# One attention-score kernel: the first of twelve input loads made in two transfers, rows 0 to 111 and rows 112 to 127

## The chip, the core and the metric

The kernel runs on one core of a Trainium2 chip. The metric is the device time of one execution in microseconds (us), the median of several runs; lower is better. The profile is one execution recorded by the hardware profiler.

## The reference

```python
def reference(x, y):      # x, y: (8, 12, 512, 64) float32
    return np.einsum('bhtc,bhsc->bhts', x, y).astype(np.float32)
```

For each of 96 heads, the 512 x 64 matrix x is multiplied by the transpose of the 512 x 64 matrix y. The output has 96 matrices of 512 x 512 in float32. 25.2 MB are read and 100.7 MB are written.

## The kernel before, in words

The 96 heads are taken in six groups of 16 (NG = 6). A group's x, and likewise its y, is one tile of 128 partitions by 4096 floats: 128 rows of 16 KB, 2 MB, contiguous in memory. So there are twelve loads, x and y in turn (load n is x of group n // 2 for even n, y for odd n). There are 48 outputs of 2 MB, each a tile of the same shape, 128 x 4096 floats. Loads and outputs share five slots in SBUF (`slots`, line 61); a slot is handed out in turn by `slot()` (line 123).

Each group goes through these steps:

- `load(n)` (line 127) issues the transfer of one tile into a slot on SyncE's DMA queue (line 131).
- `compress(n)` (line 136) casts it to bf16: x by one copy on ACT into `xk`, y by four copies on DVE, POOL and ACT into `yb`.
- `mix` (line 160) arranges x in `xb`, `transposes` (line 175) turns both in blocks of 32 x 32 on DVE, into `xT` and `yT`.
- `products` (line 197) makes four matmuls into half of PSUM, and `result` (line 221) copies each half to the output's slot, nearly always on ACT.
- `store` (line 211) sends the slot out, every third output (and the last four) on ACT's queue and the others on SyncE's.

All is written by hand in one order, and `emit` (line 86) adds the waits. It keeps for each buffer who wrote it last and who has read it since, and has the next instruction wait on those semaphores. A DMA into or out of slot i counts on the slot's own semaphore, `dma{i}`, which rises by 16 with each transfer (`step`, line 93); a reader waits for the count that stood after the last write. `writes=both(i)` is what makes a load the writer of both halves of slot i.

Near the change the order is this: lines 246 and 247 issue loads 0 to 4 back to back on SyncE, into the five empty slots. Nothing is waited for. Then two memsets, and `compress(0)`, the first reader of slot 0, on ACT (line 113 within `copy`). When load 0 is compressed, load 5 goes into slot 0, and so on. The loop of line 255 does the twelve loads; the first outputs are made in between.

At the end, line 278 has five engines wait for the last transfers of the five slots.

Of the kernel before, what the change touches and what calls it, by code (L numbers as in the profile page):

```python
# [9 lines left out]
def kernel(  # L10
# [22 lines left out]
    nc = tc.nc  # L33
    B, H, T, C = x.shape
    _, _, S, _ = y.shape
    P = 128
# [16 lines left out]
    xv = x.rearrange("b h t c -> (b h t c)").rearrange("(g p n) -> g p n", p=P, n=R * C)  # L53
    yv = y.rearrange("b h t c -> (b h t c)").rearrange("(g p n) -> g p n", p=P, n=R * C)
# [6 lines left out]
    slots = [sb.tile([P, K * S], fp32, name=f"slot{i}") for i in range(SLOTS)]  # L61
# [9 lines left out]
    def need(name, points):  # L71

        best = {}
        for p, v in points:
            if known[name].get(p, 0) < v:
                best[p] = max(best.get(p, 0), v)
        for p, v in list(best.items()):
            if any(snaps[q, w].get(p, 0) >= v for q, w in best.items() if q != p):
                del best[p]
        for p, v in best.items():  # L80
            engines[name].wait_ge(sems[p], v)  # L81
            known[name][p] = v
            for q, w in snaps[p, v].items():
                known[name][q] = max(known[name].get(q, 0), w)

    def emit(name, make, reads=(), writes=(), dma=None):

        points = [writer[r] for r in (*reads, *writes) if r in writer]
        points += [v for w in writes for v in readers.get(w, ())]
        if name == "pool" and name in ticks:  # L90
            points.append((name, ticks[name]))
        need(name, points)
        p, step = (name, 1) if dma is None else (f"dma{dma}", 16)
        if p not in sems:
            sems[p] = tc.alloc_semaphore(p)
        make().then_inc(sems[p], step)
        at = (p, ticks.get(p, 0) + step)
        ticks[p] = at[1]
        snaps[at] = {**known[name], p: at[1]}
        if dma is None:  # L100
            snaps[at][name] = at[1]
        for r in reads:
            readers.setdefault(r, []).append(at)
        for w in writes:
            writer[w], readers[w] = at, []
# [14 lines left out]
    def both(i):  # L120
        return [("slot", i, 0), ("slot", i, 1)]

    def slot():
        made_slots.append(len(made_slots) % SLOTS)
        return made_slots[-1]

    def load(n):
        i = loaded[n] = slot()
        emit(
            "sp",  # L130
            lambda: nc.sync.dma_start(slots[i], (yv if n % 2 else xv)[n // 2]),  # L131
            writes=both(i),
            dma=i,
        )

    def compress(n):

# [107 lines left out]
    with tc.tile_critical():  # L245
        for g in range(SLOTS):
            load(g)
        for half, name in enumerate(("dve", "pool")):
# [3 lines left out]
                writes=[("xb", half, part) for part in range(4)],  # L252
            )
        front = []
        for n in range(2 * NG):
            if n == 11:
                result(3, slot())
            compress(n)
            mix(n // 4, "pool", n % 4)
            if n == 4:  # L260
                transposes(0)
            if n < 5:
                load(n + SLOTS)
            elif n in (6, 8):
                load(n // 2 + 7)
            elif n < 10:
                front.append(slot())
            if n > 7 and n < 11:
                result(n - 8, front[n - 8])
            if n == 9:  # L270
                transposes(1)
# [38 lines left out]
```

## Time and profile before

| | |
|---|---|
| time, median of 3 runs | 300.91 us (300.87 to 301.03) |
| span of the profiled execution, first to last instruction | 299.3 us |
| ACT busy | 204.2 us, 68% |
| DVE busy | 160.8 us, 54% |
| PE busy | 131.2 us, 44% |
| POOL busy | 56.0 us, 19% |
| moved by DMA | 125.90 MB, 421 GB/s over the span |
| the loads, issue to landing | median 17.6 us (x), 20.8 us (y) |
| the stores, issue to landing | median 17.0 us (SyncE's queue), 14.8 us (ACT's) |

The profile gives the span of the recorded execution; the time that the runs report includes 1.6 us more around it (300.91 less 299.3). The page cuts the span into 40 slices of 7.48 us, and gives for each the busy tenths of every engine, the mean busy share of the core's 16 DMA engines and the GB/s that they moved. A window does the same for any stretch; a packet that the DMA engines move is booked in the window in which it starts, so a share can stand above 1. "SPq" and "ACTq" are the instructions with which SyncE and ACT issue a transfer. Behind the views, the trace keeps the start and the duration of each DMA packet (here one packet is one row of 16 KB), and the times at which the semaphore of a slot rose. Times are counted from the start of the span.

### The profile page before, as it was taken

What the parts mean: (1) busy time and instruction counts of PE and PEld (TensorE: products, weight loads), DVE (VectorE), ACT (ScalarE), POOL (GpSimd) and SP (SyncE); (2) the same over time, 40 slices, a digit from 0 to 9 for tenths busy, and PEclk for the clock granted to TensorE, in tenths of its full rate; (3) what the DMA queues carried; (4) which work ended last, traced back from release to release, by engine and by line L of the source; (5) the groups of instructions that cost most, each with busy time, mean ns of one, the idle gap of its engine ahead of it and who ended that gap; (6) DMA issues with size and microseconds to landing.
All of it is one profiled execution on the core that took longest, in us unless ns stands there. A gap on an engine that the chain in (4) does not pass through costs nothing.

```text
span 299.3 us, 1170 instructions
## 1 busy us (share of the span) xinstructions
PE 131.2 (44%) x384; PEld 35.2 (12%) x384; DVE 160.8 (54%) x77; ACT 204.2 (68%) x105; POOL 56.0 (19%) x23
## 2 busy tenths in 40 slices
PE   0000040557756665454655545464646473755100
PEld 0000010111111111111111111111111111111000
DVE  2167897999839590940946729219276330501400
ACT  1665676999999885677776868595959595459000
POOL 2399999991000000000000000000000000000000
PEclk9999999999599978596859597959597959587755
DMA  7999999999999999999999999999999999999995
GB/s 272 429 427 434 431 425 427 429 431 427 434 434 429 429 431 428 431 434 431 427 434 428 429 434 429 429 427 436 425 425 429 427 434 423 425 423 429 431 431 239
DMA packets 8645, 125.90 MB, mean 421 GB/s; under 512 B 960, under 2 KB 960, under 8 KB 960
## 3 DMA queue, kind: packets, MB, share of 16 engines
q1 hardware_dynamic: 6048, 88.08, 69.3%
q10 hardware_dynamic: 2592, 37.75, 29.6%
q8 instruction: 3, 0.05, 0.1%
q14 instruction: 2, 0.02, 0.0%
HBM read 25.17 MB, written 100.66 MB: 420 GB/s over the span
## 4 chain that ended last, share of the span: by engine, by line
DMA 57%; ACT 22%; PE 7%; issue 4%; DVE 3%; SPq 0%; ACTq 0%
DMA out_dram<-slot 44%; ACT slot L113 19%; DMA slot<-in_y_dram 7%; PE pm L202 7%; DMA slot<-in_x_dram 6%; DVE yb L115 2%; DVE slot L115 1%; ACT xk L113 1%; ACT yb L113 1%; SPq L131 0%; ACTq L81 0%; SPq L305 0%; SPq L245 0%
## 5 line engine op out<-in xcount | busy, mean ns | idle before, releaser
L113 ACT ACTIVATE slot<-pm 128x2048 f32<-128x2048 f32 x92 | 166.6, 1883 | 50.1 <-DMA out_dram<-slot 40.8
L202 PE MATMUL pm<-yT,xT 128*128 128x512 bf16 x384 | 131.2, 485 | 146.6 <-ACT slot L113 108.6
L180 DVE STREAM_TRANSPOSE xT<-xb 128x2048 uint32<-128x2048 uint32 x12 | 46.7, 3890 | 71.0 <-PE pm L202 68.6
L202 PEld LDWEIGHTS pm<-yT,xT 128*128 128x128 bf16 x384 | 35.2, 112 | 242.1 <-ACT slot L113 141.4
L115 DVE COPY xb<-xk 32x2048 bf16<-32x2048 bf16 x36 | 46.9, 1304 | 1.0
L115 DVE CAST yb<-slot 64x2048 bf16<-64x2048 f32 x12 | 36.1, 3012 | 17.0 <-DMA slot<-in_y_dram 16.8
L115 POOL COPY xb<-xk 32x2048 bf16<-32x2048 bf16 x12 | 36.2, 3019 | 10.5 <-ACT xk L113 9.7
L113 ACT ACTIVATE xk<-slot 128x4096 bf16<-128x4096 f32 x6 | 21.7, 3617 | 16.4 <-DMA slot<-in_x_dram 16.4
L115 DVE COPY slot<-pm 128x2048 f32<-128x2048 f32 x4 | 9.0, 2286 | 29.3 <-PE pm L202 29.3
L189 DVE STREAM_TRANSPOSE yT<-yb 128x1024 uint32<-128x1024 uint32 x12 | 23.2, 1932 | 0.0
L113 ACT ACTIVATE yb<-slot 64x2048 bf16<-64x2048 f32 x6 | 14.8, 2461 | 5.1 <-DMA slot<-in_y_dram 5.1
L115 POOL CAST yb<-slot 64x2048 bf16<-64x2048 f32 x6 | 17.8, 2968 | 1.3 <-DMA slot<-in_y_dram 0.8
L251 DVE MEMSET xb<- 128x2048 uint32 x1 | 1.8, 1765 | 1.4 <-SPq L245 1.4
L251 POOL MEMSET xb<- 128x2048 uint32 x1 | 1.8, 1804 | 0.5 <-SPq L245 0.5
L113 ACT ACT_TABLE_LOAD x1 | 1.3, 1283 | 0.9 <-SPq L245 0.9
L294 POOL MEMSET const-float32-0.0<- 128x1 f32 x1 | 0.1, 98 | 0.2 <-issue 0.2
L294 POOL MEMSET const-float32-1.0<- 128x1 f32 x1 | 0.1, 98 | 0.0
L294 POOL MEMSET const-bfloat16-1.0<- 128x1 bf16 x1 | 0.1, 98 | 0.0
L294 POOL MEMSET const-uint8-127<- 128x1 uint8 x1 | 0.1, 97 | 0.0
## 6 DMA issues: line engine op xcount, KB each, us to landing
out_dram<-slot SPq DMA_DIRECT2D x30, 2048.0 KB, 17.0
out_dram<-slot ACTq DMA_DIRECT2D x18, 2048.0 KB, 14.8
slot<-in_x_dram SPq DMA_DIRECT2D x6, 2048.0 KB, 17.6
slot<-in_y_dram SPq DMA_DIRECT2D x6, 2048.0 KB, 20.8
```

The source lines that it names most:

```text
L113: lambda: nc.scalar.activation(dst, src, COPY)
L115: else engines[name].tensor_copy(dst, src),
L180: lambda: nc.vector.transpose(xTs[half].rearrange("p (k r e) -> p k e r", k=K, e=E), xbs[half].rearrange("p (k e c) -> p k e c", k=K, e=E),),
L189: lambda: nc.vector.transpose(yTs[half].rearrange("p (r j) -> p j r", r=D), ybs[half][b].rearrange("p (j c) -> p j c", c=D),),
L202: last = nc.tensor.matmul(pms[k // 4][:, j, :], xT[:, k + j, h, :], yT[:, h * S:(h + 1) * S], start=True, stop=True,)
L251: lambda: engines[name].memset(xbs[half], 0.0),
L294: nc = _bacc.Bacc("TRN2", target_bir_lowering=False, num_devices=1)
```

## The change

Load 0 is made in two transfers on the same queue and with the same semaphore, rows 0 to 111 (14 of 16 parts of the tile, 1.75 MB) and rows 112 to 127 (256 KB). Only the second is marked as the slot's writer; since the semaphore then stands at 32, `compress(0)` waits for both. The eleven other loads are as before.

```diff
     def load(n):
         i = loaded[n] = slot()
-        emit(
-            "sp",
-            lambda: nc.sync.dma_start(slots[i], (yv if n % 2 else xv)[n // 2]),
-            writes=both(i),
-            dma=i,
-        )
+        edges = (0, 7 * P // 8, P) if n == 0 else (0, P)
+        for lo, hi in zip(edges, edges[1:]):
+            emit(
+                "sp",
+                lambda: nc.sync.dma_start(slots[i][lo:hi], (yv if n % 2 else xv)[n // 2, lo:hi]),
+                writes=both(i) if hi == P else [],
+                dma=i,
+            )
```

## The prediction

> **What bounds the kernel now.** I read the page's slices first, then the DMA table, the windows over the first microseconds, the order of time there, and the list of the DMA queue's own waits. The two DMA lines of the slices:
>
> ```profile
> DMA  7999999999999999999999999999999999999995
> GB/s 272 429 427 434 431 425 427 429 431 427 434 434 429 429 431 428 431 434 431 427 434 428 429 434 429 429 427 436 425 425 429 427 434 423 425 423 429 431 431 239
> ```
>
> The 16 DMA engines are busy from the second slice to the last but one, at 423 to 436 GB/s, whatever the other engines do. The busiest of those, ACT, is at 68%. So the end is set by bytes: 125.9 MB at some 430 GB/s. The trace's records of single packets say the same for one engine: 480 data packets of 16 KB, nearly all of 608 to 621 ns, median 611, each starting as the one before it ends. 480 x 0.61 us is 293 us, and the packets run from 1.98 to 297.84 us. Only three things can move the time: when full speed begins, what one engine's 480 packets take, and the few us after the last of them. A delay to one engine's packets early on is never made good, for its later packets queue behind it without a hole; it reaches the end whole if that engine is among the last to finish.
>
> The start is the one stretch below full speed that the change touches. In the windows the last two numbers are the DMA share and GB/s, both booked where a packet starts:
>
> ```profile
> 2.00:2.25 0.25, 0.00 (x0) 0.00 (x0) 0.25 (x1) 0.18 (x1) 0.25 (x1) 1.00 4.44 786
> 2.25:2.50 0.25, 0.00 (x0) 0.00 (x0) 0.25 (x1) 0.00 (x0) 0.25 (x1) 1.00 0.71 131
> 2.50:2.75 0.25, 0.00 (x0) 0.00 (x0) 0.25 (x1) 0.00 (x0) 0.25 (x1) 1.00 0.79 131
> 2.75:3.00 0.25, 0.00 (x0) 0.00 (x0) 0.25 (x1) 0.00 (x0) 0.00 (x0) 1.00 0.32 66
> 3.00:3.25 0.25, 0.00 (x0) 0.00 (x0) 0.21 (x1) 0.00 (x0) 0.00 (x0) 1.00 0.24 66
> 3.25:3.50 0.25, 0.00 (x0) 0.00 (x0) 0.00 (x0) 0.00 (x0) 0.00 (x0) 1.00 0.00 0
> 3.50:4.50 1.00, 0.00 (x0) 0.00 (x0) 0.00 (x0) 0.00 (x0) 0.00 (x0) 1.00 1.01 426
> ```
>
> Sixteen first packets start between 1.98 and 2.45, four engines start a second one before 3.03, and then none starts until 3.50; from there on the rate is full. In the packet records those first packets took 712 to 1956 ns in place of 611, and four second ones 959 to 1673. The first load lands at 8.79 us by its semaphore, 6.81 us after the first packet; the next lands 4.87 us later. So some 1.9 us are lost at the start, a ceiling for what any change there can gain.
>
> **The order around the change.** SyncE hands out the five loads like this (columns: start, duration, queue, line):
>
> ```profile
> 0.95 0.39 SPq L131 DMA_DIRECT2D slot<-in_x_dram  x1
> 1.40 0.42 SPq L131 DMA_DIRECT2D slot<-in_y_dram  x1
> ...
> 1.86 0.43 SPq L131 DMA_DIRECT2D slot<-in_x_dram  x1
> 2.33 0.66 SPq L131 DMA_DIRECT2D slot<-in_y_dram  x1
> 3.04 0.49 SPq L131 DMA_DIRECT2D slot<-in_x_dram  x1
> 8.81 3.62 ACT L113 ACTIVATE xk<-slot 128x4096 bf16<-128x4096 f32 x1 [6.63 <-DMA slot<-in_x_dram]
> ```
>
> **The change part by part.**
>
> *One more issue on SyncE.* The first issue is cut in two and the four other loads are pushed back by one issue, 0.39 to 0.66 us by these rows. SyncE's next instruction is the load at 12.46, which waits for ACT's xk, so the queue absorbs it. The DMA engines have the 112 rows, some 7 x 0.61 = 4.3 us of work each, before they need the next transfer; the second issue is out within 0.7 us. Nothing waits. If that cover were gone the cost would be one issue, 0.4 us.
>
> *An earlier start.* The first packet comes 0.63 us after the end of the first issue. If issue time goes with rows, 112 rows save an eighth of 0.39 us, 0.05 us. If it does not, nothing. I take zero.
>
> *16 more completion packets,* one for each engine. Their records are 7 to 9 ns, and a load's spacing of 4.87 to 4.89 us is 8 x 0.607 = 4.86 us of rows (packets overlap by about 4 ns) plus 0.01 to 0.03. I take +0.03 us.
>
> *The wait for load 0.* ACT's compress now waits for both transfers. Behind it on ACT stand the other copies; POOL's first mix waits for ACT's xk. If load 0 lands d later, slot 0 comes free d later and the load issued at 12.46 comes d later. It is needed only when the four loads behind are through, at 28.34 us by their semaphore: 15.9 us of cover. The tightest later place is 51.59, where a load is issued while transfers to 57.7 are still queued: 6 us of cover, and the delayed transfers shift with it. So the wait costs nothing by itself.
>
> *How the rows fall on the engines.* This is the disputed part. A 128-row transfer gives each engine 8 rows; they run without hindering one another, else 611 ns would not be the time of nearly every packet at all skews. 112 rows are 7 each and 16 rows are 1 each, so the bytes per engine are as before, if the division is even. But the 16 rows are neighbours, partitions 112 to 127 of one tile, and all 16 engines write them at about the same time as soon as they are through with their seven. The trace has no 16-row transfer. Bounds: nothing, if writes to neighbouring rows don't hinder one another (0.61 us for the row, which engine and row had before); and all sixteen one after another, 16 x 0.61 = 9.8 us, so +9.2. Below nothing: at most the 1.9 us of the slow start, if the other division of rows dissolves it. The nearest row is the one moment at which sixteen engines start together on one transfer and do hinder one another, the first packets: the slowest took 1956 ns, as if 3.2 engines shared one way. The end belongs to the slowest engine, so I take 1.956 - 0.611 = **+1.35 us** for the second transfer, as an estimate from that row.
>
> The Trainium skill speaks against the change here: "SBUF — State Buffer", section "Door 1: The DMA port swizzle (why `[64,N]` ≈ `[32,N]`)", says that a transfer's rate goes with how many of 16 ports its partitions reach, and has 104 GB/s for sixteen partitions, which reach four. By that the 256 KB would take 2.52 us in place of 0.61, +1.91 us, and the time would be 302.9 (an estimate from that page). The page measured a transfer by itself; no run here shows it yet, and the 611 ns of the 128-row transfers neither bear it out nor speak against it.
>
> The same doubt hangs on the seven-row shares. In the best case they fall as before and cost nothing; if engines met in twos for all seven rows, it would be 7 x 0.61 = +4.3 us. Full-speed packets of every 128-row transfer are the nearest row, so I take nothing and keep the upper end.
>
> *Sum:* 0 (issue) + 0 (start) + 0.03 + 0 (wait) + 1.35 + 0 = +1.38 us. Against the profiled execution's span of 299.3 that is 300.7. The median of the runs, 300.91, is 1.6 us above the span; what lies around the span does not change, so the forecast is 300.91 + 1.38 = **302.3 us**.
>
> **The rivals.**
>
> *A. It costs next to nothing.* The rows land as before, only the issue and the completions are added. For it: equal bytes for each engine, and a queue that is never empty. The upper end: the start's stall ends at 3.50 and SyncE's last issue at 3.53; if the stall is caused by the issues, a sixth makes it 0.42 us longer. Against that: the issue at 12.46 slows no packet. 300.9 to 301.4, middle 301.1.
>
> *B. Faster.* The first sixteen packets of a 128-row transfer hinder one another, 1.9 us lost in all. If that comes from which rows the engines start on together, shares of seven begin at other addresses and could be rid of it. It decides as soon as it returns more than the second transfer costs. Price: half of 1.9 us, 299.9 us. Against it: the stall ends for all engines at nearly one moment, 3.5, which looks like a start-up cost that any first transfer pays.
>
> *C. Seven-row shares collide too.* Half of the 4.3 us above, beside the 1.35: 304.4 us. For it: the change makes all shares start at uneven rows. Against it: engines out of step avoid one another after a collision.
>
> *D. The change does nothing on the chip* is out: the order of instructions has both transfers on SyncE and is otherwise the same on every engine.
>
> **How the numbers follow.** Forecast (301.6 to 303.2): 0.48. A: 0.24. B: 0.18. C and beyond: 0.10. Within 0.2% of 300.91 is 300.31 to 301.51, about what a measurement of this kernel can tell from no change; so faster 0.18, same 0.24, slower 0.58. The range goes from 300.0, which holds A and the edge of B, to 304.4, the middle of C; outside are some 0.14 of B and 0.05 of C.
>
> **What would show it.** In the changed profile the first load's landing, and so the start of ACT's first xk, moves from 8.81 to about 10.2; the windows between 6 and 10 us hold a dip to a quarter or a half of 430 GB/s; the last slices keep their 423 to 436 and the span grows by what the dip lost. If ACT still starts at 8.8 with a longer span, the row step is wrong. If the windows from 2.25 to 3.50 fill up, B is right. A first slice unchanged and a changed tail would mean that the end is set by something that I do not see.

## The result and the profile after

The changed kernel takes **304.67 us** (median of 4 runs, 304.63 to 305.29) against 300.97 (4 runs, 300.87 to 301.21) for the kernel before: +3.70 us, a ratio of 1.0126 (95% interval 1.0114 to 1.0138). The sign was forecast, the size was not: the forecast was 302.3, and the range ended at 304.4.

The span of the profiled execution goes from 299.3 to 302.8 us. Its slices, DMA share and GB/s:

```profile
DMA  7999999999999999999999999999999999999996
GB/s 214 307 426 424 431 431 428 428 426 433 428 437 428 433 426 425 439 422 428 433 428 420 436 426 418 437 422 428 433 426 424 435 424 420 437 420 426 435 422 260
```

The first slice has 214 GB/s where it had 272, the second 307 where it had 429; from the third on the rate is what it was. The share still says 9 in that slice: the DMA engines are busy, but their packets take longer. Everything that was lost was lost before 15 us. The windows over the start of the changed kernel (the last two numbers are DMA share and GB/s; "..." stands for lines left out):

```profile
2.25:2.50 0.25, 0.00 (x0) 0.00 (x0) 0.25 (x1) 0.00 (x0) 0.25 (x1) 1.00 0.00 0
...
3.25:3.50 0.25, 0.00 (x0) 0.00 (x0) 0.00 (x0) 0.00 (x0) 0.00 (x0) 1.00 0.83 328
3.50:4.50 1.00, 0.00 (x0) 0.00 (x0) 0.00 (x0) 0.00 (x0) 0.00 (x0) 1.00 1.16 344
4.50:8.50 4.00, 0.00 (x0) 0.00 (x0) 0.00 (x0) 0.00 (x0) 0.00 (x0) 1.00 1.03 274
8.50:12.50 4.00, 0.00 (x0) 0.00 (x0) 0.00 (x0) 0.00 (x0) 0.00 (x0) 1.00 0.90 221
```

The last two of these windows in the kernel before:

```profile
4.50:8.50 4.00, 0.00 (x0) 0.00 (x0) 0.00 (x0) 0.00 (x0) 0.00 (x0) 1.00 0.99 422
8.50:12.50 4.00, 0.00 (x0) 0.00 (x0) 0.00 (x0) 3.62 (x1) 0.01 (x1) 1.00 1.00 430
```

Here the whole of load 0 is slow, not only its last eighth: 274 GB/s while the seven-row shares are written (422 before), 221 while the 16 rows follow and load 1 begins (430 before). In the packet records, the packets that start between 3.5 and 8.3 us take 971 ns in the median, those between 8.3 and 11.3 us 1300; the kernel before has a median of 611 in both stretches. The excess over 611 ns of all data packets that start before 14 us, divided by 16 engines, is 4.15 us; it was 0.97. That is +3.2 us for the mean engine; the last packet of all ends 3.55 us later than before (301.39 against 297.84).

The records also show how many rows each engine had. A packet starts some 4 ns before the one ahead of it on its engine ends, so starts and ends can be linked into chains. In the changed kernel this gives sixteen chains, and each begins with seven packets of 16 KB and one completion packet. In fourteen of them one row and its completion follow as plainly; in the other two the second completion can't be told from a neighbour's. The shares are even, and the time went into slower packets, not into an engine with more rows than the others.

What followed on the other engines, in order of time:

```profile
0.95 0.86 SPq L133 DMA_DIRECT2D slot<-in_x_dram  x2
...
1.86 0.42 SPq L133 DMA_DIRECT2D slot<-in_y_dram  x1
2.32 0.74 SPq L133 DMA_DIRECT2D slot<-in_x_dram  x1
3.10 0.52 SPq L133 DMA_DIRECT2D slot<-in_y_dram  x1
3.67 0.46 SPq L133 DMA_DIRECT2D slot<-in_x_dram  x1
12.87 3.62 ACT L113 ACTIVATE xk<-slot 128x4096 bf16<-128x4096 f32 x1 [10.69 <-DMA slot<-in_x_dram]
16.52 0.33 SPq L133 DMA_DIRECT2D slot<-in_y_dram  x1
```

ACT's first copy moves from 8.81 to 12.87, and the load that follows it from 12.46 to 16.52, 4.06 us each. No hole opens behind them.

### The profile page after: what moved, and what is told of

Read it like the earlier page. It is cut to its first block, busy times and chain, and to the rows that moved or that the text cites. A ratio compares the mean times of both kernels' runs of the same rounds, so it can differ in the third digit from the quotient of the medians.

```text
span 302.8 us, 1164 instructions
## 1 busy us (share of the span) xinstructions
PE 126.7 (42%) x377; PEld 34.8 (11%) x384; DVE 161.3 (53%) x77; ACT 204.0 (67%) x105; POOL 56.2 (19%) x23
## 4 chain that ended last, share of the span: by engine, by line
DMA 56%; ACT 21%; PE 6%; DVE 5%; issue 4%; SPq 1%; ACTq 0%; DVEq 0%
DMA out_dram<-slot 41%; ACT slot L113 19%; DMA slot<-in_y_dram 8%; PE pm L204 6%; DMA slot<-in_x_dram 6%; DVE yb L115 2%; DVE slot L115 1%; DVE xT L182 1%; ACT xk L113 1%; ACT yb L113 1%; SPq L133 1%; DVE yT L191 1%; ACTq L81 0%; SPq L307 0%; DVEq L81 0%
## 5 line engine op out<-in xcount | busy, mean ns | idle before, releaser
L204 PE MATMUL pm<-yT,xT 128*128 128x512 bf16 x377 | 126.7, 475 | 154.7 <-ACT slot L113 106.4
```

Of the source, the lines that this page charges most:

```text
L204: last = nc.tensor.matmul(pms[k // 4][:, j, :], xT[:, k + j, h, :], yT[:, h * S:(h + 1) * S], start=True, stop=True,)
```

## The experiments

The theory after the result: a transfer's rate is set by which partitions of the tile it writes. Engines that write neighbouring partitions at the same time share a way into the SBUF and slow one another. Its rivals: (1) a second or a short transfer costs as such; (2) the addresses that are read, or uneven shares of seven rows (the chains above speak against the uneven shares); (3) the slow start of the first transfer. Each ratio is taken against runs of the kernel before that were made beside it (medians 300.95 to 301.00).

### Cut by columns in place of rows

```diff
-        edges = (0, 7 * P // 8, P) if n == 0 else (0, P)
+        edges = (0, 7 * K * S // 8, K * S) if n == 0 else (0, K * S)
...
-                lambda: nc.sync.dma_start(slots[i][lo:hi], (yv if n % 2 else xv)[n // 2, lo:hi]),
-                writes=both(i) if hi == P else [],
+                lambda: nc.sync.dma_start(slots[i][:, lo:hi], (yv if n % 2 else xv)[n // 2][:, lo:hi]),
+                writes=both(i) if hi == K * S else [],
```

> Load 0 is again made in two transfers of seven eighths and one eighth of its bytes, but cut by columns: both have all 128 rows. Theory (which partitions a transfer names decides; neighbouring ones share a way into the SBUF): no dip, the rows fall as in the kernel before, +0.03 to +0.1 us for one more row start and completion per engine: 300.9 to 301.4. Rival 1 (a second transfer in the first load, or a short one, costs as such): as the changed kernel, 304.0 to 305.0. Rival 2 (shares of seven rows begin at unlucky addresses in the memory that is read): 300.9 to 301.4 too, since every engine has 8 rows.

Measured: **300.94 us**, ratio 1.0000 (0.9991 to 1.0009). The same two transfers of seven eighths and one eighth cost nothing when both have all 128 rows. Rival 1 falls: neither the sixth issue, nor 16 completions more, nor a transfer of one eighth of the bytes costs anything that can be measured here.

### Two halves of 64 rows

```diff
-        edges = (0, 7 * P // 8, P) if n == 0 else (0, P)
+        edges = (0, P // 2, P) if n == 0 else (0, P)
```

> Load 0 in two transfers of 64 rows: four rows for each engine, twice. Theory: all rows of the first transfer lie in one half of the tile, so engines meet in twos at least on every row, 8 x 0.61 = +4.9 us at most: 304.7 to 305.9, not less than the changed kernel. Rival 1 (an extra transfer, the shorter the worse): less than the changed kernel, 301 to 303. Rival 2 (uneven shares of seven rows): about as before, 300.9 to 301.5. The Trainium skill, SBUF - State Buffer, section on Door 1, has partitions 0 to 63 reach half of the ports, which makes it +4.9 by that page (an estimate).

Measured: **305.74 us**, +4.79, ratio 1.0155 (1.0140 to 1.0170); above the change, though the shares are even and neither piece is short. Its windows:

```profile
4.00:6.00 2.00, 0.00 (x0) 0.00 (x0) 0.00 (x0) 0.00 (x0) 0.00 (x0) 1.00 1.04 213
6.00:8.00 2.00, 0.00 (x0) 0.00 (x0) 0.00 (x0) 0.00 (x0) 0.00 (x0) 1.00 0.89 197
8.00:10.00 2.00, 0.00 (x0) 0.00 (x0) 0.00 (x0) 0.00 (x0) 0.00 (x0) 1.00 1.19 246
10.00:12.00 2.00, 0.00 (x0) 0.00 (x0) 0.00 (x0) 0.00 (x0) 0.00 (x0) 1.00 0.83 172
```

The rate is about half of 430 GB/s for as long as load 0 lasts, and the packets that start from 3.8 to 11 us take 1279 ns in the median, 2.09 x 611, as if engines met in twos on every row. Eight rows at twice the time would be 8 x 0.61 = +4.9 us; the excess of the packets before 14 us is 5.15 us per engine against 0.97, so +4.2. Another 0.35 us has a different source: an issue of 64 rows takes 0.59 us in place of 0.39, and the first packet starts at 2.33 us in place of 1.98.

By the Trainium skill ("SBUF — State Buffer", section "Door 1: The DMA port swizzle (why `[64,N]` ≈ `[32,N]`)") partitions 0 to 63 reach 8 of 16 ports; this run agrees, with +4.79 us and 1279 ns.

### Even and odd rows

```diff
-        edges = (0, 7 * P // 8, P) if n == 0 else (0, P)
-        for lo, hi in zip(edges, edges[1:]):
+        parts = (0, 1) if n == 0 else (None,)
+        for part in parts:
+            rows = slice(part, P, 2) if n == 0 else slice(0, P)
...
-                lambda: nc.sync.dma_start(slots[i][lo:hi], (yv if n % 2 else xv)[n // 2, lo:hi]),
-                writes=both(i) if hi == P else [],
+                lambda: nc.sync.dma_start(slots[i][rows], (yv if n % 2 else xv)[n // 2, rows]),
+                writes=[] if part == 0 else both(i),
```

> Load 0 in two transfers of 64 rows again, but one has the even rows and the other the odd ones, so that each spreads over the whole tile. Theory in its strict form (an engine takes a run of rows of the transfer's own list, here 4 rows that lie 2 apart, and every engine still meets another on every row): as with the lower and upper half, 305 to 306. Theory in a loose form (it is enough that a transfer spreads over the tile): 300.9 to 301.6.

Measured: **301.47 us**, +0.47, ratio 1.0015 (1.0005 to 1.0024). Two transfers of 64 rows again, as many bytes and issues, but each spread over the whole tile: nine tenths of the 4.79 us are gone. Most of the 0.47 that is left fits the later first packet (2.34 us in place of 1.98), as with the halves. The windows at the same place (418 and 451 GB/s in the kernel before):

```profile
4.00:6.00 2.00, 0.00 (x0) 0.00 (x0) 0.00 (x0) 0.00 (x0) 0.00 (x0) 1.00 0.98 410
6.00:8.00 2.00, 0.00 (x0) 0.00 (x0) 0.00 (x0) 0.00 (x0) 0.00 (x0) 1.00 1.03 442
```

So it is which rows a transfer has, not how many. In this pair of runs the rows read and the partitions written change together; the next runs part the two. The strict form of the theory, that every engine takes a run of the transfer's own list and so meets another here too, falls.

### Sixteen rows more, in three forms

The kernel before, load 0 whole, and behind it one transfer of 16 rows into slot 4, which load 4 overwrites after a wait. It adds 256 KB, one row per engine, 0.61 us.

```diff
         for g in range(SLOTS):
             load(g)
+            if g == 0:
+                emit(
+                    "sp",
+                    lambda: nc.sync.dma_start(slots[4][112:128], xv[0, 112:128]),
+                    writes=both(4),
+                    dma=4,
+                )
```

The second form writes `slots[4][0:128:8]`, and the third writes neighbouring partitions again but reads `xv[0, 0:128:8]`.

> The kernel before, with load 0 whole, and behind it one transfer more: the rows 112 to 127 of load 0 once again, into the neighbouring partitions 112 to 127 of slot 4, which load 4 then overwrites (load 4 waits for it; SyncE's queue has 10 us to spare). The bytes alone are one row per engine, +0.61 us, 301.6. Theory: four engines share a way, +0.61 and 1.2 to 1.9 more: 302.7 to 303.5. Rival 1 (a short transfer costs as such) the same. Rival 3 (the price was only that of the start, where the first transfer is slow anyway): 301.6.

> As the run with one more transfer of 16 rows, the same 16 rows read, but written to every eighth partition (0, 8, ... 120) of slot 4. Theory: fewer engines meet, bytes +0.61 and 0 to 0.7 more: 301.5 to 302.3, at least 0.7 us below its twin. Rival 1 (a short transfer costs as such) and rival 2 (the addresses read): as its twin, within 0.3 us.

> As the run with 16 rows more into partitions 112 to 127 of slot 4 (303.87), but read from every eighth row of load 0's tile in memory, so that only the addresses read are spread. Theory (the written partitions decide): 303.5 to 304.2. Rival 2 (the addresses read decide): 302.2 to 302.7, as its twin that was spread on the written side.

| 16 rows | us | above before | beyond the bytes |
|---|---|---|---|
| neighbours read, neighbours written | 303.87 | +2.92, ratio 1.0097 (1.0080 to 1.0113) | 2.3 |
| spread read, neighbours written | 303.76 | +2.79, ratio 1.0086 (1.0071 to 1.0101) | 2.2 |
| neighbours read, every eighth written | 302.44 | +1.49, ratio 1.0050 (1.0035 to 1.0065) | 0.9 |

For 16 rows, spreading what is read changes nothing that can be measured; spreading what is written takes 1.4 us off. The windows around the extra rows, first neighbours written, then every eighth:

```profile
8.00:10.00 2.00, 0.00 (x0) 0.00 (x0) 0.00 (x0) 0.00 (x0) 0.00 (x0) 1.00 0.99 139
10.00:12.00 2.00, 0.00 (x0) 0.00 (x0) 0.00 (x0) 1.58 (x1) 0.00 (x0) 1.00 0.71 270
```

```profile
8.00:10.00 2.00, 0.00 (x0) 0.00 (x0) 0.00 (x0) 0.81 (x1) 0.00 (x0) 1.00 1.00 279
10.00:12.00 2.00, 0.00 (x0) 0.00 (x0) 0.00 (x0) 2.00 (x1) 0.00 (x0) 1.00 0.96 410
```

The dip of the first is to a third of full rate, and lasts into the next window; that of the second is to two thirds. The slowest packets around the extra rows take 2.33 us with neighbours, 3.8 x 0.611, and 1.17 us with every eighth, 1.9 x 0.611: as if four engines met in the first form and two in the second. Rival 2, as far as it meant the addresses read, falls for 16 rows, and rival 3 too: a whole load went ahead of these rows. The first and the second form came out 0.1 to 0.4 us above what the theory had as its upper end (303.5 and 302.3).

### The 112 rows by themselves

The same edit with `slots[4][0:112], xv[0, 0:112]`, and as a control with `slots[4], xv[0]`.

> The kernel before, load 0 whole, and behind it rows 0 to 111 of load 0 once again into partitions 0 to 111 of slot 4 (load 4 overwrites them after a wait). The bytes alone are 7 rows per engine, 7 x 0.61 = +4.27 us: 305.2. Theory (seven-row shares collide as well, 3.7 us of the change less the 2.3 us that 16 neighbouring rows cost beyond their bytes leaves 1.4): 306.3 to 307.5. Rival (only the 16 neighbouring rows collide): 305.0 to 305.4.

> Control for the run with 112 rows more: all 128 rows of load 0 once again into slot 4. Bytes 8 x 0.61 = +4.9 us, and no collision by any theory: 305.6 to 306.0. Theory: below the run with 112 rows more, though it moves 256 KB more. Rival (only the 16 neighbouring rows collide): 0.6 us above it.

Measured: **308.46 us** for 112 rows more (+7.49, ratio 1.0248, 1.0233 to 1.0264), **305.87** for 128 rows more (+4.90, ratio 1.0162, 1.0147 to 1.0177). The transfer with 256 KB less takes 2.6 us more. The windows while the added rows move, first with 112 rows, then with 128:

```profile
8.00:10.00 2.00, 0.00 (x0) 0.00 (x0) 0.00 (x0) 0.21 (x1) 0.00 (x0) 1.00 1.08 279
10.00:12.00 2.00, 0.00 (x0) 0.00 (x0) 0.00 (x0) 2.00 (x1) 0.00 (x0) 1.00 0.94 221
12.00:14.00 2.00, 0.00 (x0) 0.00 (x0) 0.00 (x0) 1.41 (x1) 0.53 (x1) 1.00 1.14 336
14.00:16.00 2.00, 0.00 (x0) 0.00 (x0) 0.00 (x0) 0.00 (x0) 1.91 (x1) 1.00 0.97 254
```

```profile
8.00:10.00 2.00, 0.00 (x0) 0.00 (x0) 0.00 (x0) 1.10 (x1) 0.00 (x0) 1.00 1.01 434
10.00:12.00 2.00, 0.00 (x0) 0.00 (x0) 0.00 (x0) 2.00 (x1) 0.00 (x0) 1.00 0.94 401
12.00:14.00 2.00, 0.00 (x0) 0.00 (x0) 0.00 (x0) 0.52 (x1) 1.42 (x1) 1.00 1.07 459
14.00:16.00 2.00, 0.00 (x0) 0.00 (x0) 0.00 (x0) 0.00 (x0) 1.02 (x1) 1.00 0.99 426
```

128 rows cost their bytes, 8 x 0.61; 112 rows cost 7 x 0.61 = 4.27 and 3.2 us beyond. The expectation had 1.4, from subtracting 2.3 from the change's 3.7; the two collisions do not add up, 3.2 + 2.3 = 5.5 against 3.7 when one follows the other. The reads were not varied for 112 rows; that the written partitions decide there too is carried over from the 16 rows, not shown.

### At load 2 in place of load 0, and the small piece first

```diff
-        edges = (0, 7 * P // 8, P) if n == 0 else (0, P)
+        edges = (0, 7 * P // 8, P) if n == 2 else (0, P)
```

> The change's own cut, rows 0 to 111 and 112 to 127, at load 2 in place of load 0, with ten microseconds of full-rate transfers ahead of it. Theory (where in the order makes little difference): +2.8 to +4.0 us, 303.8 to 305.0. Rival 3 (the price comes from the slow start of the first transfer): at most +0.6, 300.9 to 301.6.

Measured: **305.22 us**, +4.25, ratio 1.0140 (1.0123 to 1.0157). Ten microseconds into full rate, the same cut costs no less. Rival 3 falls altogether. That it costs half a microsecond more than at load 0 is not certain, as the two intervals overlap.

```diff
-        edges = (0, 7 * P // 8, P) if n == 0 else (0, P)
+        edges = (0, P // 8, P) if n == 0 else (0, P)
```

> The change's cut the other way round: rows 0 to 15 first, then rows 16 to 127. The two prices measured apart are +3.2 us (seven-row shares, 7.5 less the 4.27 of their bytes) and +2.3 us (16 neighbouring rows, 2.92 less 0.61), the change cost 3.7, less than their sum. Theory (partitions decide; what is saved against the sum comes from engines that reach the second piece out of step): here all engines meet in the 16 rows first, so between the change and the sum: 304.7 to 306.5. Rival 1 (a short transfer at the end of the load holds the load up): less than the change, 301 to 303.5.

Measured: **304.25 us**, +3.25, ratio 1.0103 (1.0086 to 1.0120). Both expectations missed: it is 0.4 us below the change, where the theory had it above, and well above what the rival allowed. The order of the two pieces matters little, and the argument from the sum of the two prices was wrong. Its interval overlaps that of the change, so that it is cheaper is not certain.

### Small packets first

The cut by columns with `K * S // 8`: 128 rows of 2 KB, then 128 rows of 14 KB.

> Load 0 cut by columns with the small piece first: 128 rows of 2 KB, then 128 rows of 14 KB. Theory: no collision, 300.8 to 301.3. If the slow first two microseconds came from the sixteen 16 KB packets that start together (rival B of the prediction), small packets first would shorten them and give up to 1 us back: 299.9 to 300.6.

Measured: **301.47 us**, +0.47, ratio 1.0012 (1.0003 to 1.0021). No gain; the slow first two microseconds do not come from the size of the packets that start together. Most of its 2 KB packets take 84 ns, but several that start before 3.5 us take 0.8 to 1.5 us. It came out 0.5 us above the other cut by columns; their intervals just overlap, and the reason is not known.

No experiment pointed to a version faster than the kernel before.

## Why the prediction was wrong, point by point

- **What bounds the kernel: right.** Time lost by the DMA engines in the first 13 us came out at the end: ACT's first copy 4.06 us later, the last packet 3.55 us, the time 3.70 us. 4.9 us of added packets (128 rows more) gave +4.90.
- **One more issue, an earlier start, 16 completions: right, near nothing.** The cut by columns adds the issue and the completions, and gives 300.94. Issuing the 112 rows takes 0.39 us, as 128 did, and the first packet starts at 1.97 us (1.98 before).
- **The wait for load 0: right.** It was late by 4 us of its 15.9 us of cover, and no later slice shows a hole.
- **The 16 neighbouring rows: right in kind, too small.** Taken +1.35 us from the slowest first packet; 2.3 us by itself. The row it was taken from shows the start, which the spread transfers pay as well (excess over 611 ns of the packets that start before 3.5 us: 0.95 us per engine before, 0.65 with even and odd rows), so it was no measure of this collision. The sentence beside it, which took +1.91 from the Trainium skill ("SBUF — State Buffer", section "Door 1: The DMA port swizzle (why `[64,N]` ≈ `[32,N]`)"), was nearer: 2.3 measured.
- **The seven-row shares: this is the step that failed.** "In the best case they fall as before and cost nothing ... Full-speed packets of every 128-row transfer are the nearest row, so I take nothing and keep the upper end." They cost 3.2 us by themselves, about as much as the whole change. The 128-row packets were no evidence on it: they show that eight-row shares of a full tile don't collide, and say nothing of how 112 rows are dealt out. It was the condition of rival C, to which the chances gave 0.10. That C's 304.4 came so near to 304.67 is luck: it had 2.15 for the seven-row shares and 1.35 for the 16 rows, where 3.2 and 2.3 were measured apart, and the two do not add up when one follows the other.
- **Rival B: wrong, though its sign came in part.** The windows from 2.25 to 3.50 hold 14 starting packets in place of 6. But the excess of the packets that start before 3.5 us, 0.72 us per engine against 0.95, is no gain that can be told apart: runs that leave load 0 whole have 0.67 to 0.95 there. The 1.9 us taken as its ceiling was the loss of the last engine; the slow packets come to those 0.95 us per engine. (Its price, 300.91 less half of 1.9, is 300.0, not 299.9.)
- **The sign of the forecast came in part too.** A dip between 6 and 10 us was there, but it began with load 0's first rows, at 262 GB/s in the window from 4 to 6 us, and ACT's first copy moved to 12.87 in place of about 10.2.

**What is shown:** the price comes from cutting load 0 by rows (the cut by columns is free), not from the number of transfers, their size or the place in the order; adjoining rows cost it and spread rows hardly do; and for 16 rows it is the partitions written that decide, not the addresses read. **What stays open:** why 112 rows cost 3.2 us beyond their bytes. The chains show seven rows for each engine, but the packet records name neither engine nor row, so which partitions meet is not known, and a part of the reads is not excluded there. The Trainium skill's port rule ("SBUF — State Buffer", section "Door 1: The DMA port swizzle (why `[64,N]` ≈ `[32,N]`)") by itself doesn't give it: by its table 112 partitions still reach all 16 ports, twelve of them with eight rows, so 8 x 0.61 in place of 7 x 0.61, +0.6 us (an estimate from that page), where 3.2 us were measured. Engines whose seven rows straddle the page's groups of four could meet more often; that is argued, not shown.

## What to carry to other kernels

In a kernel bound by DMA, cut a transfer by columns (all 128 partitions in each piece), not by rows: here the first cost nothing and the second 3.7 us, once. A piece that must have fewer partitions should be spread over the tile: 64 even rows ran at full rate, 64 adjoining ones at half; 16 rows at every eighth partition still lost 0.9 us, against 2.3 for neighbours. And a duration taken from full transfers is no price for a partial one; where the trace has none of that shape, the bound belongs in the forecast, not beside it.

## What the runs showed that I had not expected

- 112 rows take longer than 128: 7.49 us against 4.90 as an addition to the same queue.
- A DMA share of 9 tenths or more in a slice does not mean full rate: in the changed kernel's second slice it stands over 307 GB/s. GB/s beside the share tells a slow packet from a busy engine.
- For 16 rows, reading neighbouring rows in place of spread ones cost nothing (303.87 and 303.76 us); writing neighbouring partitions in place of every eighth cost 1.4 us (303.87 and 302.44).
